# Sixteen rounds of cached value pages in a decoder step: neighbouring rounds, four weight tiles, two row groups

## The chip, the cores and the metric

The kernel runs on one core of a Trainium2 chip. The metric is the time of one launch on the device, in microseconds (us); the time before is the median of three runs. The core has a matrix engine (PE, with its weight loads shown apart as PEld), a vector engine (DVE), an activation engine (ACT), a general engine (POOL) and SyncE (SP), which here only issues transfers. Each engine works through its own queue in order and waits on semaphores.

## The reference

One layer of a decoder step on two groups of tokens at once: a prompt of 256 tokens, and 8 sequences with 4 new tokens each (32 "sample" tokens). 288 tokens in all, 2048 features, float32 throughout.

```
h = h + 1/2 * SwiGLU(RMSNorm(h))                     # FFN 1, hidden 5632
h = h + W_out[ norm(conv group) | norm(attention) ]  # 1024 conv features | 8 heads x 128
h = h + 1/2 * SwiGLU(RMSNorm(h))                     # FFN 2
h = h + sigmoid(W_g RMSNorm(h)) * (W_p p)
y = RMSNorm(h)
```

The attention of the sample tokens runs over a paged past and over the new tokens themselves:

```
k_past = cache_k[page_table]; v_past = cache_v[page_table]     # 8 sequences x 8 pages x 128 rows
s = q k_all^T * SCALE + F_t - F_s                              # forgetting bias, causal
o = softmax(s) @ concat(v_past, v_new)                         # per sequence and head
```

So 64 value pages (128 rows x 8 heads x 128 floats, 512 KB each) have to be gathered and multiplied with the probabilities, and after them the values of the 32 new tokens.

## The kernel before

Activations are kept with features on the 128 partitions and the 288 tokens along the free axis. Each float32 product with a weight is made of three products of a faster type: weight and activation are split into a high and a low part. A weight comes as a block of 512 rows x 256 columns (512 KB, tile `wraw`, tags `raw0` to `raw7`), is split by ACT (`whi`, L271) and DVE (`wlo`, L272) in halves, and one *chunk* of PE work (L304 to L306, 24 matmuls of 288 columns) uses it. `split_upto` keeps five halves ahead of PE.

Weights and value pages are listed in one sequence, `items`. `load_upto` requests them up to a fixed number of items ahead of the point that PE's program has reached (`AHEAD`, 12, in the stage of the pages). Weights are requested on SP's queue (L237), pages as indirect transfers on POOL's queue (L247). A requested tile waits until the former tile of the same tag has been read for the last time. A framework below the kernel places the semaphores, and a planner orders each engine's queue at build time by estimated times: it takes the instruction that is first in the program among those it thinks ready.

*Value pages.* A round `v_round(gi, r)` handles page number `r` (0 to 7) of the four sequences of group `gi` (0 or 1): it has four pages and eight matmuls, two halves `e` of four heads each, by four column tiles of 32 (one a sequence), and adds into two PSUM banks `va`. Rounds are numbered 0 to 15 here, group 0 first, and pages 0 to 63, four a round. There are eight page buffers, taken in turn by `page_tile`: `raw4` to `raw7`, which the weights give up while pages come (`WEIGHTS` is 4), three of their own (`v0` to `v2`) and `wideb`. Page n reuses, in the main, the buffer of page n - 8; at the start the order is shifted, since `wideb` isn't free yet: page 7 takes page 0's buffer, page 11 takes that of page 4 (`v0`).

After round 7 and after round 15 `sample_out` adds the new tokens' part (`vs`, eight matmuls with 32 rows, L750), and DVE picks each head's own rows; `sample_turn` transposes the result (L765). `natural` writes the new tokens' values into `vs` while the value projection runs, and `probs_t` turns the probabilities into `PT`, the weights of the rounds.

*The order.* The chunks of this stage are a list `fill`: 0 to 15 the key projection, 16 to 51 conv, 52 to 67 the value projection, 68 to 79 conv, 80 to 95 the conv half of the output projection. Everything else is hung into it by hand with `at(i, ...)`: it is put before chunk i. Round r stands at `int(51 + 2.7 * r)`: 51, 53, 56, 59, 61, 64, 67, 69, 72, 75, 78, 80, 83, 86, 88, 91. The attention heads of the prompt (`prompt_head`, eight from 69 to 86; their masks on POOL, transposes L814 three chunks later) stand there too. Then the attention half of the output projection follows, and FFN 2.

The weights' tag is chosen as

```
state["wslot"] = (state["wslot"] + 1) % (WEIGHTS if 0 < state["pages"] < 2 * DB * PAGES // 2 else RAW)
```

where `state["pages"]` counts the pages requested so far: from the first page requested to the last one there are four weight tiles, before and after eight.

Of the kernel before, what the change touches and what calls it, by code (L numbers as in the profile page):

```python
# [16 lines left out]
F32 = mybir.dt.float32  # L17
# [79 lines left out]
def build(nc, tc, ctx, A, O):  # L97
# [121 lines left out]

    steps = []  # L220
    items = []
    state = dict(wslot=0, pages=0, ahead=RAW, loaded=0, split=0, used=0, halves_used=0, chunk=0, lead=HALVES)

    def load_upto(n):
        while state["loaded"] < min(n, len(items)):
            it = items[state["loaded"]]
            if it["kind"] == "p" and "vx" not in W:
                return
            if it["kind"] == "w":
                state["wslot"] = (state["wslot"] + 1) % (WEIGHTS if 0 < state["pages"] < 2 * DB * PAGES // 2 else RAW)  # L230
                t = rawp.tile([P, it["nk"], 256], F32, name="wraw", tag=f"raw{state['wslot']}")
                src = it["src"].rearrange("(k p) c -> p k c", p=P)
                if state["loaded"] == 0:
                    tc.keep_in_program_order(sy.dma_start(t[:, :2], src[:, :2]))
                    d = sy.dma_start(t[:, 2:], src[:, 2:])
                else:
                    d = sy.dma_start(t, src)  # L237
                if state["used"] < 24:
                    tc.keep_in_program_order(d)
            elif it["kind"] == "k":  # L240
                t = W["kt"][0].tile([P, 4, NH, P], F32, name="KT", tag="KT", bufs=2)
                for i, r in enumerate(it["rows"]):
                    g.indirect_dma_start(out=t[:, i].rearrange("p h s -> p (h s)"), out_offset=None, in_=it["src"],  # L243
                                         in_offset=bass.IndirectOffsetOnAxis(ap=r, axis=0))
            else:
                t = page_tile()
                g.indirect_dma_start(out=t, out_offset=None, in_=it["src"],  # L247
                                     in_offset=bass.IndirectOffsetOnAxis(ap=it["rows"], axis=0))
            it["tile"] = t
            state["loaded"] += 1  # L250
# [372 lines left out]
    def v_evac(i):  # L623
        def evac(b, o):
            hh = 2 * i + b
            t = W["cv"][0].tile([P, NT], F32, name="tB", tag="tB", bufs=3)
            v.tensor_tensor(t, o, rs, ALU.mult)

            def out():
                c = slice(hh * P, hh * P + P)  # L630
                natural(M["vn"][:, :, c], M["vs"][:, c], t)
            defer(out)
        return evac

# [78 lines left out]
    def probs_t(gi):  # L713
        pt = wide(*(("vv", "c"), ("mix", "a"))[gi], f"PT{gi}")
        x = M["s", gi]
        for j in range(2):
            t = ktbank()
            for i in range(4):
                c = (4 * j + i) * P
                pe.transpose(t[:, i * P:i * P + P], x[:, c:c + P], ident)  # L720
            for b in range(4):
                v.tensor_copy(pt[:, j * 512:j * 512 + 512].rearrange("s (i b c x) -> s b i c x", i=4, b=4, c=4)[:, b],
                              t.rearrange("s (i c b x) -> s b i c x", i=4, c=4, b=4)[:, b])
        t = ktbank()
        pe.transpose(t[:NS, :P], x[:, PAGES * P:], ident)
        for b in range(4):
            v.tensor_copy(pt[:NS, 8 * P + 32 * b:8 * P + 32 * b + 32].rearrange("s (c x) -> s c x", x=8),
                          t[:NS, :P].rearrange("s (c b x) -> s b c x", c=4, b=4)[:, b])
        M["PT", gi] = pt

    def v_round(gi, r):
        its = [page(A["cache_v"], (4 * gi + b) * PAGES + r) for b in range(4)]

        def fn():
            if r == 0:
                M["va", gi] = [bank("va", BANKS["va"]) for _ in range(2)]
                M["pv", gi] = M["PT", gi].rearrange("s (r b x) -> s r b x", b=4, x=32)
            for e in range(2):
                for b in range(4):
                    pe.matmul(M["va", gi][e][32 * b:32 * b + 32, :], M["pv", gi][:, r, b],  # L740
                              its[b]["tile"][:, e * 512:e * 512 + 512], start=r == 0, stop=False, tile_position=(0, 32 * b))
            if r == PAGES - 1:
                sample_out(gi)
        return (its, fn)

    def sample_out(gi):
        mx = W["vv"][0]
        for e in range(2):
            for b in range(4):
                pe.matmul(M["va", gi][e][32 * b:32 * b + 32, :], M["pv", gi][:NS, 8, b],  # L750
                          M["vs"][:, e * 512:e * 512 + 512], start=False, stop=True, tile_position=(0, 32 * b))
        o = mx.tile([P, P], F32, name="so", tag="so", bufs=2)
        for hh in range(NH):
            src = M["va", gi][hh // 4][:, hh % 4 * P:hh % 4 * P + P]
            m = const("headmask")[:, hh:hh + 1]
            if hh == 0:
                v.tensor_scalar(o, src, m, None, ALU.mult)
            else:
                v.scalar_tensor_tensor(o, src, m, o, ALU.mult, ALU.add)
        defer(lambda: sample_turn(gi, o))  # L760

    def sample_turn(gi, o):
        mx = W["vv"][0]
        t = ktbank()
        pe.transpose(t[:, :P], o, ident)  # L765
        for half in range(2):
            v.tensor_copy(M["oS"][:, 4 * half:4 * half + 4, 16 * gi:16 * gi + 16].rearrange("p c (b t) -> p c b t", t=DT),
                          t[:, :P].rearrange("p (b c a t) -> p a c b t", c=4, a=2, t=DT)[:, half])
        if gi == 1:
            s.dma_start(O["v_prompt"].rearrange("(j p) c -> p j c", p=P), M["vn"])  # L770
            s.dma_start(O["v_sample"], M["vs"])
            for hh in range(NH):
                split(za[hh][0][:, SEQ:], za[hh][1][:, SEQ:], M["oS"][:, hh, :], gain("norm_attn_out", hh))
            sq = mx.tile([P, NH, NS], F32, name="sqS")
            s.activation(sq, M["oS"], AF.Square)
            v.tensor_reduce(acc[:, SEQ:], sq.rearrange("p h n -> p n h"), AX.X, ALU.add)
# [130 lines left out]
    def v_start():  # L907
# [5 lines left out]
        state["ahead"] = AHEAD  # L913
        vv = W["vv"][0]
        M["vn"] = vv.tile([P, 2, NH * P], F32, name="vn")
        M["vs"] = vv.tile([NS, NH * P], F32, name="vs")
        M["oS"] = vv.tile([P, NH, NS], F32, name="oS")

    def between(fill, marks):
# [26 lines left out]
    def at(i, *fns):  # L946
        marks.setdefault(i, []).extend(fns)
# [39 lines left out]
    at(50, lambda: probs_t(0))  # L987
    at(52, lambda: probs_t(1))
    for r in range(2 * PAGES):
        at(int(51 + VSTEP * r), v_round(r // PAGES, r % PAGES))  # L990
    for hh in range(NH):
        at(int(69 + 2.5 * hh), lambda hh=hh: prompt_head(hh))
    at(80, lambda: norm_scale(rsc, acc2, CB * P, 2))
# [138 lines left out]
```

## Time and profile before

| what | before |
|---|---|
| median of 3 runs | 2338.74 us (2338.55 to 2339.37) |
| profiled execution | 2338.26 us, its span 2336.5 us |
| granted clock of PE, mean | 0.997 |
| value rounds, L740 | 256 records, first start 1106.9 us, last 1285.5 us |
| new tokens' part, L750 | 32 records, 1184.2 us and 1286.5 us |
| transfers over the span | 443.52 MB, mean 190 GB/s |

A row of the timeline reads: start in us, length in us, engine, line, operation, output<-inputs, shape (rows * columns of weights, then output), count, and in brackets the idle time of the engine before it with what ended it. A row of waits reads: who waited <- for whom: us in total, times, longest. A row of windows reads: stretch, its length, the busy time of each engine with its instructions in brackets, the granted clock, the busy share of the transfer engines and GB/s. A row of a transfer queue reads: packets, MB, share of the 16 engines. A float32 matmul with page data shows as two records, one a pass, so a round of eight matmuls shows as x16.

### The profile page before, as it was taken

Reading aid. Unit: us, or ns where it says so; the run is one execution under the profiler, and the core shown is the slowest. Engines: PE = TensorE matmul, PEld = TensorE weight load, DVE = VectorE, ACT = ScalarE, POOL = GpSimd, SP = SyncE. Lnnn points to the kernel's source line nnn. Section 1 sums busy time; section 2 is a strip of 40 time slices with the busy share of each in tenths; the row PEclk is TensorE's granted clock in tenths of the full one; section 3 lists DMA queues with packets and bytes.
Section 4 is the critical chain, followed back from the end, with each engine's and each line's share of the span. In section 5 each row is a group of like instructions: output and inputs, shape, how many; then the busy total and the mean of one; then the engine's idle time right before and its main releaser. Section 6 shows DMA issues by size and latency. Waiting matters only on the chain.

```text
span 2336.5 us, 44258 instructions
## 1 busy us (share of the span) xinstructions
PE 2319.3 (99%) x17390; PEld 2256.6 (97%) x17390; DVE 1338.8 (57%) x2386; ACT 1054.9 (45%) x1857; POOL 334.0 (14%) x403
## 2 busy tenths in 40 slices
PE   9999999999999999999999999999999999999997
PEld 9999999999999999888888999999999999999997
DVE  6555555555555585455566765555555555555755
ACT  7444444444444553333344554444444444444654
POOL 2020000000000113444445210000000000000111
PEclk9999999999999999999999999999999999999999
DMA  8575555555555557998998455555555555555552
GB/s 273 162 239 164 167 166 163 166 166 165 162 165 167 164 160 230 333 311 260 327 312 284 154 164 156 178 154 174 168 163 163 167 166 164 163 167 166 163 170 86
DMA packets 391089, 443.52 MB, mean 190 GB/s; under 512 B 17104, under 2 KB 371424, under 8 KB 390880
## 3 DMA queue, kind: packets, MB, share of 16 engines
q1 hardware_dynamic: 369456, 366.89, 50.6%
q0 software_dynamic: 20384, 71.38, 8.8%
q8 instruction: 136, 2.23, 0.4%
q10 hardware_dynamic: 1040, 2.42, 0.3%
q14 instruction: 73, 0.60, 0.1%
HBM read 435.56 MB, written 5.07 MB: 189 GB/s over the span
## 4 chain that ended last, share of the span: by engine, by line
PE 99%; DVE 0%; DMA 0%; ACT 0%; DVEq 0%; issue 0%; ACTq 0%
PE mm L304 31%; PE mm L306 31%; PE mm L305 30%; PE va L740 1%; PE va L683 1%; PE va L306 1%; PE va L304 1%; PE va L305 1%; PE kt L180 0%; PE kt L304 0%; PE kt L306 0%; PE kt L305 0%; DVE h L1067 0%; DMA gT<-in_gains_dram 0%; DMA wraw<-in_w_out_dram 0%; PE kt L790 0%
## 5 line engine op out<-in xcount | busy, mean ns | idle before, releaser
L272 DVE TENSOR_TENSOR wlo<-wraw,whi 128x512 fp32r<-128x512 f32 x1384 | 971.5, 706 | 802.4 <-ACT whi L271 749.0
L271 ACT ACTIVATE whi<-wraw 128x512 fp32r<-128x512 f32 x1384 | 865.3, 630 | 948.5 <-PE mm L305 879.3
L304 PE MATMUL mm<-xh,whi 128*128 128x288 f32 x3680 | 1094.8, 297 | 0.0
L305 PE MATMUL mm<-xl,whi 128*128 128x288 f32 x3680 | 1085.6, 295 | 0.0
L306 PE MATMUL mm<-xh,wlo 128*128 128x288 f32 x3680 | 1082.2, 294 | 0.0
L304 PEld LDWEIGHTS mm<-xh,whi 128*128 128x128 f32 x3680 | 689.5, 187 | 23.2 <-issue 20.2
L306 PEld LDWEIGHTS mm<-xh,wlo 128*128 128x128 f32 x3680 | 692.9, 188 | 0.1
L305 PEld LDWEIGHTS mm<-xl,whi 128*128 128x128 f32 x3680 | 690.8, 188 | 0.2
L304 PE MATMUL mm<-hh,whi 128*128 128x288 f32 x1408 | 416.8, 296 | 0.0
L305 PE MATMUL mm<-hl,whi 128*128 128x288 f32 x1408 | 415.4, 295 | 0.0
L306 PE MATMUL mm<-hh,wlo 128*128 128x288 f32 x1408 | 414.0, 294 | 0.0
L370 POOL TENSOR_TENSOR sr<-sg,rs 128x288 f32<-128x288 f32 x88 | 72.4, 823 | 1407.7 <-ACT sg L368 1407.6
L306 PEld LDWEIGHTS mm<-hh,wlo 128*128 128x128 f32 x1408 | 265.2, 188 | 0.0
L305 PEld LDWEIGHTS mm<-hl,whi 128*128 128x128 f32 x1408 | 264.3, 188 | 0.0
L304 PEld LDWEIGHTS mm<-hh,whi 128*128 128x128 f32 x1408 | 263.7, 187 | 0.0
L390 DVE SCALAR_TENSOR_TENSOR h<-mm,h 128x288 f32<-128x288 f32 x192 | 87.2, 455 | 23.3 <-PE mm L306 22.9
L215 POOL TENSOR_TENSOR acc<-acc,sq 128x288 f32<-128x288 f32 x59 | 51.1, 866 | 248.5 <-ACT sq L214 245.6
L243 POOL DMA_INDIRECT KT<-in_cache_k_dram,idx x64 | 66.0, 1032 | 122.7 <-PE va L683 54.2
L368 ACT ACTIVATE sg<-tg 128x288 f32<-128x288 f32 x88 | 39.0, 444 | 97.8 <-DVE tg L366 97.7
L377 ACT ACTIVATE hh<-hd 128x288 fp32r<-128x288 f32 x88 | 39.2, 446 | 92.8 <-DVE hd L375 92.8
L247 POOL DMA_INDIRECT page<-in_cache_v_dram,idx x64 | 64.5, 1008 | 71.3 <-PE va L740 49.4
L378 DVE TENSOR_TENSOR hl<-hd,hh 128x288 fp32r<-128x288 f32 x88 | 40.8, 464 | 22.1 <-ACT hh L377 22.1
(232 smaller groups left out, 1329.9 us busy)
## 6 DMA issues: line engine op xcount, KB each, us to landing
wraw<-in_w_ffn_up_dram SPq DMA_DIRECT2D x176, 512.0 KB
wraw<-in_w_ffn_gate_dram SPq DMA_DIRECT2D x175, 512.0 KB
wraw<-in_w_ffn_down_dram SPq DMA_DIRECT2D x160, 512.0 KB
wraw<-in_w_in_dram SPq DMA_DIRECT2D x96, 512.0 KB
wraw<-in_w_out_dram SPq DMA_DIRECT2D x32, 512.0 KB
wraw<-in_w_ple_gate_dram SPq DMA_DIRECT2D x32, 512.0 KB
wraw<-in_w_ffn_down_dram SPq DMA_DIRECT2D x32, 256.0 KB
wraw<-in_w_ple_proj_dram SPq DMA_DIRECT2D x8, 256.0 KB
```

The costliest lines, as they stand in the source:

```text
L215: (v if k >= KT - last_on_v else g).tensor_tensor(acc, acc, sq, ALU.add)
L243: g.indirect_dma_start(out=t[:, i].rearrange("p h s -> p (h s)"), out_offset=None, in_=it["src"], in_offset=bass.IndirectOffsetOnAxis(ap=r ...
L247: g.indirect_dma_start(out=t, out_offset=None, in_=it["src"], in_offset=bass.IndirectOffsetOnAxis(ap=it["rows"], axis=0))
L271: s.activation(hi, x, AF.Copy)
L272: v.tensor_tensor(lo, x, hi.bitcast(F32), ALU.subtract)
L304: pe.matmul(o, hi[:, j % 2, w], xh, start=f, stop=False)
L305: pe.matmul(o, hi[:, j % 2, w], xl, start=False, stop=False)
L306: pe.matmul(o, lo[:, j % 2, w], xh, start=False, stop=l)
L370: g.tensor_tensor(r, u, rs, ALU.mult)
L377: s.activation(H["hi"][:, k, :], t, AF.Copy)
L378: v.tensor_tensor(H["lo"][:, k, :], t, H["hi"][:, k, :].bitcast(F32), ALU.subtract)
L390: v.scalar_tensor_tensor(h[:, k, :], o, 0.5, h[:, k, :], ALU.mult, ALU.add)
```

## The change

Four edits. Round r of group 0 moves so that rounds 1 and 2, 3 and 4, 5 and 6 stand at one place each, and of group 1 so that 8 and 9, 10 and 11, 12 and 13, 14 and 15 do: 51, 56, 56, 61, 61, 67, 67, 69, then 75, 75, 80, 80, 86, 86, 91, 91. Weights stay on four tiles until the code of the last round has been written (`through`), instead of until the last page has been requested; then they go on with `raw4`. The new tokens' values `vs` are kept with heads 0 to 3 on partitions 0 to 31 and heads 4 to 7 on partitions 32 to 63, the probabilities of the new tokens are copied to both, and the eight matmuls of `sample_out` alternate between the two row groups. The output `v_sample` is therefore written by two transfers. `page_tile`, `AHEAD` and all else are as before.

```diff
--- before.py
+++ after.py
@@ -219,7 +219,7 @@
 
     steps = []
     items = []
-    state = dict(wslot=0, pages=0, ahead=RAW, loaded=0, split=0, used=0, halves_used=0, chunk=0, lead=HALVES)
+    state = dict(wslot=0, pages=0, through=False, ahead=RAW, loaded=0, split=0, used=0, halves_used=0, chunk=0, lead=HALVES)
 
     def load_upto(n):
         while state["loaded"] < min(n, len(items)):
@@ -227,7 +227,7 @@
             if it["kind"] == "p" and "vx" not in W:
                 return
             if it["kind"] == "w":
-                state["wslot"] = (state["wslot"] + 1) % (WEIGHTS if 0 < state["pages"] < 2 * DB * PAGES // 2 else RAW)
+                state["wslot"] = (state["wslot"] + 1) % (WEIGHTS if state["pages"] and not state["through"] else RAW)
                 t = rawp.tile([P, it["nk"], 256], F32, name="wraw", tag=f"raw{state['wslot']}")
                 src = it["src"].rearrange("(k p) c -> p k c", p=P)
                 if state["loaded"] == 0:
@@ -628,7 +628,8 @@
 
             def out():
                 c = slice(hh * P, hh * P + P)
-                natural(M["vn"][:, :, c], M["vs"][:, c], t)
+                r = NS * (hh // 4)
+                natural(M["vn"][:, :, c], M["vs"][r:r + NS, hh % 4 * P:hh % 4 * P + P], t)
             defer(out)
         return evac
 
@@ -723,9 +724,10 @@
                               t.rearrange("s (i c b x) -> s b i c x", i=4, c=4, b=4)[:, b])
         t = ktbank()
         pe.transpose(t[:NS, :P], x[:, PAGES * P:], ident)
-        for b in range(4):
-            v.tensor_copy(pt[:NS, 8 * P + 32 * b:8 * P + 32 * b + 32].rearrange("s (c x) -> s c x", x=8),
-                          t[:NS, :P].rearrange("s (c b x) -> s b c x", c=4, b=4)[:, b])
+        for e in range(2):
+            for b in range(4):
+                v.tensor_copy(pt[NS * e:NS * e + NS, 8 * P + 32 * b:8 * P + 32 * b + 32].rearrange("s (c x) -> s c x", x=8),
+                              t[:NS, :P].rearrange("s (c b x) -> s b c x", c=4, b=4)[:, b])
         M["PT", gi] = pt
 
     def v_round(gi, r):
@@ -740,15 +742,18 @@
                     pe.matmul(M["va", gi][e][32 * b:32 * b + 32, :], M["pv", gi][:, r, b],
                               its[b]["tile"][:, e * 512:e * 512 + 512], start=r == 0, stop=False, tile_position=(0, 32 * b))
             if r == PAGES - 1:
+                if gi == 1:
+                    state.update(through=True, wslot=WEIGHTS - 1)
                 sample_out(gi)
         return (its, fn)
 
     def sample_out(gi):
         mx = W["vv"][0]
-        for e in range(2):
-            for b in range(4):
-                pe.matmul(M["va", gi][e][32 * b:32 * b + 32, :], M["pv", gi][:NS, 8, b],
-                          M["vs"][:, e * 512:e * 512 + 512], start=False, stop=True, tile_position=(0, 32 * b))
+        for b in range(4):
+            for e in range(2):
+                rows = slice(NS * e, NS * e + NS)
+                pe.matmul(M["va", gi][e][32 * b:32 * b + 32, :], M["pv", gi][rows, 8, b], M["vs"][rows], start=False, stop=True,
+                          tile_position=(NS * e, 32 * b))
         o = mx.tile([P, P], F32, name="so", tag="so", bufs=2)
         for hh in range(NH):
             src = M["va", gi][hh // 4][:, hh % 4 * P:hh % 4 * P + P]
@@ -768,7 +773,8 @@
                           t[:, :P].rearrange("p (b c a t) -> p a c b t", c=4, a=2, t=DT)[:, half])
         if gi == 1:
             s.dma_start(O["v_prompt"].rearrange("(j p) c -> p j c", p=P), M["vn"])
-            s.dma_start(O["v_sample"], M["vs"])
+            for e in range(2):
+                s.dma_start(O["v_sample"][:, 512 * e:512 * e + 512], M["vs"][NS * e:NS * e + NS])
             for hh in range(NH):
                 split(za[hh][0][:, SEQ:], za[hh][1][:, SEQ:], M["oS"][:, hh, :], gain("norm_attn_out", hh))
             sq = mx.tile([P, NH, NS], F32, name="sqS")
@@ -913,7 +919,7 @@
         state["ahead"] = AHEAD
         vv = W["vv"][0]
         M["vn"] = vv.tile([P, 2, NH * P], F32, name="vn")
-        M["vs"] = vv.tile([NS, NH * P], F32, name="vs")
+        M["vs"] = vv.tile([2 * NS, NH * P // 2], F32, name="vs")
         M["oS"] = vv.tile([P, NH, NS], F32, name="oS")
 
     def between(fill, marks):
@@ -987,7 +993,7 @@
     at(50, lambda: probs_t(0))
     at(52, lambda: probs_t(1))
     for r in range(2 * PAGES):
-        at(int(51 + VSTEP * r), v_round(r // PAGES, r % PAGES))
+        at(int(51 + VSTEP * (min(PAGES - 1, (r + 1) // 2 * 2) if r < PAGES else r | 1)), v_round(r // PAGES, r % PAGES))
     for hh in range(NH):
         at(int(69 + 2.5 * hh), lambda hh=hh: prompt_head(hh))
     at(80, lambda: norm_scale(rsc, acc2, CB * P, 2))
```

## The prediction

> **What bounds the kernel now.** I read the page first, then the timeline of PE in the stage of the value pages, the waits of the queues there, the DMA counters of short windows and the clock by windows.
>
> ```profile
> PE 2319.3 (99%) x17390; PEld 2256.6 (97%) x17390; DVE 1338.8 (57%) x2386; ACT 1054.9 (45%) x1857; POOL 334.0 (14%) x403
> PE 99%; DVE 0%; DMA 0%; ACT 0%; DVEq 0%; issue 0%; ACTq 0%
> ```
>
> The first line is busy time by engine, the second the chain that ended last. Both are PE for 99%, and after the value pages PE stays the chain: a microsecond won or lost on PE in that stage reaches the end whole. So I look only for what PE spends there.
>
> One isolated round, with the weight loads that show its inner steps:
>
> ```profile
> 1127.62 0.29 PE L305 MATMUL mm<-xl,whi 128*128 128x288 f32 x1
> 1127.76 0.29 PE L306 MATMUL mm<-xh,wlo 128*128 128x288 f32 x1
> 1127.98 1.92 PE L740 MATMUL va<-page,PT 128*32 128x512 f32 x16
> 1129.84 0.40 PE L304 MATMUL mm<-xh,whi 128*128 128x288 f32 x1
> 1130.07 0.29 PE L305 MATMUL mm<-xl,whi 128*128 128x288 f32 x1
> ...
> 1106.92 0.16 PEld L740 LDWEIGHTS va<-page,PT 128*32 128x32 f32 x8 [0.17 <-issue]
> 1107.38 0.13 PEld L740 LDWEIGHTS va<-page,PT 128*32 128x32 f32 x4 [0.30 <-issue]
> 1107.81 0.13 PEld L740 LDWEIGHTS va<-page,PT 128*32 128x32 f32 x4 [0.30 <-issue]
> ```
>
> Starts count here, since ends are modelled. Ordinary matmuls start every 0.133 us (1127.62 to 1127.76), so a chunk of 24 takes 3.2 us. With the round between, L306 to the second matmul after it takes 1130.07 - 1127.76 = 2.31 us where 0.27 would do: an isolated round costs 2.04 us. Inside it the four column tiles of one pass go together, and passes follow at 0.43 us (1107.38 to 1107.81): four passes are 1.72 us, and 0.32 us is the way in and out.
>
> The end of the stage:
>
> ```profile
> 1285.52 1.04 PE L740 MATMUL va<-page,PT 128*32 128x512 f32 x8
> 1286.49 1.92 PE L750 MATMUL va<-vs,PT 32*32 32x512 f32 x16
> 1290.98 0.40 PE L304 MATMUL mm<-zch,whi 128*128 128x288 f32 x1 [2.57 <-ACT whi L271]
> ...
> SPq L237 <- PE va L740: 8.9, 2, 8.0
> ACT whi L271 <- DMA wraw<-in_w_out_dram: 8.9, 1, 8.9
> ...
> 1292.20:1295.60 3.40, 3.40 (x17) 3.40 (x16) 2.49 (x7) 1.59 (x5) 0.80 (x1) 0.50 0.49 166
> 1295.60:1299.00 3.40, 3.40 (x27) 3.40 (x27) 3.31 (x11) 2.90 (x11) 0.81 (x1) 1.00 0.42 142
> ```
>
> PE stands 2.57 us after the last round. It waits for ACT's split of a weight, ACT waits for that weight's DMA, and SP had held its issue 8.0 us until a round freed the tile. The last two lines are windows (the third figure from the end is the granted clock): right behind the stall the clock is 0.50 for 3.4 us.
>
> **The change part by part.**
>
> *Weights on four tiles until the last round.* Today the eight-tile rotation starts when the last page is requested, and weights are then queued on tiles that still hold pages of rounds 14 and 15: this is the 8.0 us wait above. With four tiles they wait only for splits, as everywhere else in the stage, where PE shows no such stall. Gain: 2.57 us, and the half clock: 3.4 us x (1 - 0.133/0.24) = 1.5 us, with 0.24 us the pitch in
>
> ```profile
> 1292.86 0.24 PE mm L305
> 1293.10 0.24 PE mm L306
> ```
>
> from the chain. Together **-4.1 us**. Nothing should follow it: four raw tiles and five split halves hold about six chunks, 19 us, while rounds 14 and 15 with their finish hold PE for 5 us. SP has nothing behind the weights.
>
> *Pairs.* Rounds 1+2, 3+4, 5+6 and 8+9, 10+11, 12+13, 14+15 become neighbours; 0 and 7 stay alone. Each of seven joins saves at most the 0.32 us of one way in and out, and at least 0.18 us, if the passes at a seam keep their first-pass and last-pass gaps (0.46 and 0.53 us for 0.43). A seam of two rounds has one tile shape on both sides, like the seam of the two halves inside a round, so I take the upper: 7 x 0.32 = **-2.2 us** (bounds -1.3 and -2.2).
>
> *New tokens' values on two row groups.*
>
> ```profile
> 1182.37 1.93 PE L740 MATMUL va<-page,PT 128*32 128x512 f32 x16
> 1184.23 1.92 PE L750 MATMUL va<-vs,PT 32*32 32x512 f32 x16
> 1186.08 0.49 PE L789 MATMUL kt<-k,q 128*128 128x128 f32 x2
> ```
>
> The eight matmuls take 1.85 us, four passes of four tiles. If the two row groups go side by side, two passes are left: 2 x 0.43 = 0.86 us less, twice, **-1.7 us**. If they don't, nothing: no row here shows row groups together, so the bounds are 0 and -1.7; I take -1.7, by the four column tiles that do share 0.43 us. [...]
>
> What is added is off PE:
>
> ```profile
> L727 DVE COPY PT<-kt x8: 169/169/169, 1105.0 to 1114.9; 32x32 f32<-32x32 f32 x8
> L771 ACTq DMA_DIRECT2D out_dram<-vs x1: 374/374/374, 1182.8 to 1182.8; - x1
> ```
>
> Eight more of these copies of probabilities on DVE, 4 x 169 ns = 0.7 us a group, behind the copies that the rounds read; and one more output DMA issue of 0.37 us on ACT. DVE is busy 57%, ACT 45%, and five split halves, 8 us of PE's work, cover both. Cost 0.
>
> *What the pairs ask of the pages.* Eight page buffers, and the order in which they are reused is not changed. Page 11 (the fourth of round 2) takes the buffer of page 4 (the first of round 1), tag v0. Today three chunks lie between; now nothing does. How long a page takes:
>
> ```profile
> 1109.11 1.04 POOL L247 DMA_INDIRECT page<-in_cache_v_dram,idx  x1 [7.52 <-PE va L740]
> ...
> q0 software_dynamic: 169, 0.63, 48.0%
> ...
> 1163.16 0.94 POOL L247 DMA_INDIRECT page<-in_cache_v_dram,idx  x1 [6.97 <-PE va L740]
> 1166.89 1.34 POOL L247 DMA_INDIRECT page<-in_cache_v_dram,idx  x1 [0.30 <-issue]
> ...
> q0 software_dynamic: 576, 2.10, 52.7%
> ```
>
> The round that began at 1106.92 released POOL's issue at 1109.11, 2.19 us after its start. The first q0 line is the window 1109.1 to 1113.3: 0.63 MB, so a page (0.52 MB) is in 4.2 us after its issue. The second is 1163.1 to 1174.0: all four pages of a batch (2.10 MB), 10.8 us after the first issue. Hence (10.8 - 4.2) / 3 = 2.2 us for each further page.
>
> Page 11 is then in at 2.19 + 4.2 = 6.4 us after round 1's start; round 2 is due at 1.72. It is 4.7 us late. What PE does meanwhile depends on the planner that orders PE's queue:
>
> ```profile
> 1186.65 0.48 PE L304 MATMUL mm<-xh,whi 128*128 128x288 f32 x1
> ...
> 1190.16 0.29 PE L305 MATMUL mm<-xl,whi 128*128 128x288 f32 x1
> 1190.29 0.27 PE L765 MATMUL kt<-consts,so 128*128 128x128 f32 x1
> 1190.32 0.38 PE L306 MATMUL mm<-xh,wlo 128*128 128x288 f32 x1
> ```
>
> The program puts L765 after 12 matmuls of that chunk; it stands after 26, between two that the program writes as neighbours. So the planner fills a foreseen wait with later matmuls. I expect it to do so in round 2: page 11's two matmuls go into the next chunk, four passes alone, 4 x 0.43 + 0.32 = **+2.0 us** (upper end: PE stands, below).
>
> Round 7 is the other place. Its pages take round 5's buffers; round 5 now runs three steps later, and round 7 is due where it was. Round 6 of today, for the distance to round 7 at 1182.37 above:
>
> ```profile
> 1173.28 1.92 PE L740 MATMUL va<-page,PT 128*32 128x512 f32 x16
> ```
>
> Round 6, two chunks and a head's transposes take 9.1 us, so round 7 is due 1.72 + 9.1 = 10.8 us after round 5 starts. Its pages are in at 2.19 + 10.8 = 13.0. A wait of 2.2 us; I take **+2.2** (bounds: 0, if the pages come at the pace of a less loaded DMA, and 3.7 with the half clock behind it).
>
> The other pairs have five or six chunks. Last of eight pages: 2.2 + 4.2 + 7 x 2.2 = 21.8 us after the pair's first start; due at 2 x 1.72 + 0.3 + 16 + 1.7 = 21.4 before transposes and heads, which add 0.6 us for rounds 3 and 4 and more later. About even, 0 taken. POOL issues eight pages in a row, 10 us at 1.24 us each, with the heads' masks, the adds into h and the squares' sum queued behind; the transposes of a head come three chunks, 9.6 us, after its scores, so the masks come late by about a microsecond at worst and the planner moves the transposes: 0.
>
> Sum: -4.1 - 2.2 - 1.7 + 2.0 + 2.2 = **-3.8 us**. The profiled execution took 2338.26 us (span 2336.5), 0.5 below the median of 2338.74; from the median, **2334.9 us**.
>
> **The rivals.**
>
> *PE stands in order for page 11.* The planner goes by its own times; if it takes the page for ready, the queue keeps program order and PE waits. [...] By rows: 4.7 us of idle instead of 2.0, and since 2.57 us of idle brought the half clock, 1.5 us more: +6.2, sum +0.4, 2339.1 us. The trace agrees where it shows a wait: in the stall at 1288 nothing passed the waiting L304. For the rival: all sixteen rounds of today stand whole (x16) in program order. Against: L765.
>
> *The eight pages of a pair don't come in time (slower).* Place: rounds 4, 11 and 15, five chunks after the pair before. It decides from a page pace of about 2.6 us: then the eighth page is in at 24.6 us, after what heads and transposes add. At 3.0 us a page it is 27.4, some 4 us late, with the half clock 5.5 us, at three places +16: 2351 us; at one place 2340.4. For it: DMA is busy 0.95 to 0.99 there today,
>
> ```profile
> 1120.00:1140.00 20.00, 20.00 (x154) 18.37 (x153) 9.31 (x17) 6.89 (x11) 8.19 (x8) 1.00 0.99 342
> 1140.00:1160.00 20.00, 20.00 (x155) 16.77 (x154) 9.11 (x17) 5.64 (x10) 7.52 (x8) 1.00 0.95 315
> ```
>
> (the last two figures: DMA share, GB/s). Against: the bytes of the stage are unchanged and weights have 19 us of stock to give way.
>
> *The late pages cost nothing.* The planner moves all of round 2's second half behind a chunk and round 7's pages land 2 us earlier. Sum -8.0: 2330.7 us. For it: q0 moves a page in less where weights pause. Against: four passes for one tile alone can't be free.
>
> **How the numbers follow.** A measurement tells 0.2% from no change, 4.7 us: under 2334.1 is faster, over 2343.4 slower. Forecast (planner fills, round 7 waits): 0.50, 2332.5 to 2337; 0.17 of it is under 2334.1. PE stands: 0.20, 2336 to 2342, all same. Pairs starve: 0.15, slower in 0.12. Late pages free: 0.15, faster. Faster 0.32, same 0.56, slower 0.12. Range 2331.0 to 2342.0: below lies half of the free case, above most of the starved one.
>
> **What would show it.** After: no 2.6 us gap behind the last L750 (its line moved), no SP wait of 8 us on L740, clock 1.00 there; L750's successor in two passes, about 1 us; seven L740 groups of x32, or, if the planner fills, six and one of x28 with x4 on its own 2 to 5 us later; a wait of PE for page in round 7. The prediction is wrong if PE waits for page at rounds 4, 11 or 15, or if the row groups don't overlap.

## The result, and the profile after

The changed kernel took 2348.64 us (median of six, 2345.27 to 2351.89), the kernel before 2339.30 in the same comparison (2338.55 to 2339.97): a ratio of 1.0042, 95% interval 1.0032 to 1.0052. The forecast was 2334.9 with a range to 2342.0. So it is slower by 9.3 us, and 13.7 above the forecast. The runs of the changed kernel also lie 6.6 us apart, those of before 1.4. The profiled execution took 2351.89 us (span 2350.1).

The page, busy time and chain:

```profile
PE 2323.0 (99%) x17390; PEld 2260.1 (96%) x17390; DVE 1337.9 (57%) x2394; ACT 1054.7 (45%) x1857; POOL 331.6 (14%) x403
PE 98%; DVE 0%; issue 0%; DMA 0%; ACT 0%; another core or an unknown queue 0%; DVEq 0%; SPq 0%
```

PE still carries the chain and its count of instructions is unchanged; but a point of its share is gone, and busy ends are modelled, so the loss has to be looked for in starts. First the places that the prediction named, in PE's timeline:

```profile
1126.20 3.63 PE L742 MATMUL va<-page,PT 128*32 128x512 f32 x28
...
1132.50 1.90 PE L742 MATMUL va<-page,PT 128*32 128x512 f32 x4 [0.75 <-DMA page<-in_cache_v_dram,idx]
...
1149.82 0.29 PE L306 MATMUL mm<-xh,wlo 128*128 128x288 f32 x1
1150.04 3.64 PE L742 MATMUL va<-page,PT 128*32 128x512 f32 x32
1153.61 0.40 PE L304 MATMUL mm<-xh,whi 128*128 128x288 f32 x1
1153.85 0.29 PE L305 MATMUL mm<-xl,whi 128*128 128x288 f32 x1
...
1305.24 1.09 PE L755 MATMUL va<-vs,PT 32*32 32x512 f32 x16
1306.26 0.40 PE L304 MATMUL mm<-zch,whi 128*128 128x288 f32 x1
```

All edits did on PE what their steps said: a pair is one group of x32; rounds 1 and 2 are x28 with page 11's x4 later; the new tokens' values take 1.02 us (1305.24 to 1306.26) for 1.85; and behind the last round there is no gap. SP's wait for tiles that pages held is 1.5 us for 8.9:

```profile
SPq L237 <- PE va L742: 1.5, 2, 0.8
```

Then windows, first the three stretches of half clock, then the whole stage (the third figure from the end is the granted clock):

```profile
1187.60:1191.00 3.40, 3.40 (x19) 2.47 (x22) 1.53 (x5) 0.63 (x1) 0.00 (x0) 0.50 1.03 406
1262.70:1266.10 3.40, 3.40 (x16) 3.22 (x15) 2.50 (x8) 1.04 (x3) 2.30 (x4) 0.50 0.49 154
1290.00:1293.40 3.40, 3.40 (x17) 3.38 (x16) 3.24 (x6) 2.34 (x6) 1.23 (x2) 0.50 1.02 388
1100.00:1330.00 230.00, 217.80 (x1606) 187.19 (x1605) 130.76 (x310) 87.74 (x182) 94.69 (x115) 0.98 0.79 264
```

The one half-clock stretch of before, behind the last round, has become three at other places. PE's own waits in the stage (line, releaser, us in total, times, longest):

```profile
PE mm L304 <- issue: 2.5, 3, 1.1
PE kt L617 <- issue: 2.3, 1, 2.3
...
PE va L742 <- DMA page<-in_cache_v_dram,idx: 0.8, 1, 0.8
```

PE waits 0.8 us for pages in all. The larger waits are under "issue": nothing that the profile shows. One such place, behind the pair of rounds 3 and 4, on PE, ACT, DVE and POOL:

```profile
1148.89 0.29 PE L305 MATMUL mm<-xl,whi 128*128 128x288 f32 x1
...
1155.84 0.29 PE L305 MATMUL mm<-xl,whi 128*128 128x288 f32 x1
...
1159.04 0.29 PE L305 MATMUL mm<-xl,whi 128*128 128x288 f32 x1
...
1161.04 0.29 PE L305 MATMUL mm<-xl,whi 128*128 128x288 f32 x1
1161.47 0.29 PE L306 MATMUL mm<-xh,wlo 128*128 128x288 f32 x1
1162.91 0.39 PE L304 MATMUL mm<-xh,whi 128*128 128x288 f32 x1 [1.15 <-issue]
```

```profile
1149.22 0.63 ACT L271 ACTIVATE whi<-wraw 128x512 fp32r<-128x512 f32 x1 [2.40 <-PE mm L305]
1150.07 0.63 ACT L271 ACTIVATE whi<-wraw 128x512 fp32r<-128x512 f32 x1 [0.21 <-PE mm L305]
1158.24 0.63 ACT L271 ACTIVATE whi<-wraw 128x512 fp32r<-128x512 f32 x1 [7.54 <-PE mm L306]
1160.10 0.63 ACT L271 ACTIVATE whi<-wraw 128x512 fp32r<-128x512 f32 x1 [1.23 <-PE mm L306]
1163.81 2.20 ACT L271 ACTIVATE whi<-wraw 128x512 fp32r<-128x512 f32 x4 [3.07 <-PE mm L306]
```

```profile
1158.90 0.69 DVE L272 TENSOR_TENSOR wlo<-wraw,whi 128x512 fp32r<-128x512 f32 x1 [7.48 <-PE mm L306]
```

```profile
1152.22 0.94 POOL L247 DMA_INDIRECT page<-in_cache_v_dram,idx  x1 [14.18 <-PE va L742]
1153.46 0.94 POOL L247 DMA_INDIRECT page<-in_cache_v_dram,idx  x1 [0.30 <-issue]
...
1160.93 1.41 POOL L247 DMA_INDIRECT page<-in_cache_v_dram,idx  x1 [0.30 <-PE mm L306]
```

How to read them. Five split halves (whi and wlo) go round; ACT may write a whi once PE has read the one five before for the last time, which is an L305, the 17th or 23rd matmul of an undivided chunk. Undisturbed, ACT starts 0.33 us after that matmul starts: 1148.89, 1149.22. Behind the pair the matmul is at 1155.84 and ACT starts at 1158.24: 2.40 us. Weights were not short: the one split at 1160.10 had landed by 1148.2. Two splits later the delay is 4.77 us (the L305 at 1159.04, whi at 1163.81). The row says the same by the name it gives: the releaser should be L305, and where it is L306, PE had gone on to later matmuls before ACT was let go. The trace's record of PE's semaphore says it too: an undisturbed release is on record 0.31 us after the start of its matmul; here four fall due between 1156.1 and 1157.1, and none is on record before 1157.88. POOL's run of eight requests lasts from 1152.22 to 1162.34, just over this time. PE itself makes no progress from 1161.04 to 1162.91 but for one matmul, and not for want of halves: the two of its chunk were split by 1159.59 (ACT at 1150.07 and 1158.24, DVE's wlo at 1158.90), and the row names no one. The totals of that wait for the stage, before and after:

```profile
ACT whi L271 <- PE mm L306: 6.4, 5, 2.2
```

```profile
ACT whi L271 <- PE mm L306: 31.6, 10, 7.5
```

### The profile page after: what moved, and what is told of

Same layout as the page of the kernel before. It is cut to its first block, busy times and chain, and to the rows that moved or that the text cites. A ratio compares the mean times of both kernels' runs of the same rounds, so it can differ in the third digit from the quotient of the medians.

```text
span 2350.1 us, 44277 instructions
## 1 busy us (share of the span) xinstructions
PE 2323.0 (99%) x17390; PEld 2260.1 (96%) x17390; DVE 1337.9 (57%) x2394; ACT 1054.7 (45%) x1857; POOL 331.6 (14%) x403
## 4 chain that ended last, share of the span: by engine, by line
PE 98%; DVE 0%; issue 0%; DMA 0%; ACT 0%; another core or an unknown queue 0%; DVEq 0%; SPq 0%
PE mm L304 31%; PE mm L306 30%; PE mm L305 30%; PE va L684 1%; PE va L742 1%; PE va L304 1%; PE va L306 1%; PE va L305 1%; DMA h<-in_x_dram 0%; PE kt L796 0%; PE kt L304 0%; PE kt L306 0%; PE kt L305 0%; DVE h L1073 0%; PE kt L180 0%
## 5 line engine op out<-in xcount | busy, mean ns | idle before, releaser
L305 PE MATMUL mm<-xl,whi 128*128 128x288 f32 x3680 | 1086.1, 295 | 0.5 <-issue 0.5
L306 PE MATMUL mm<-xh,wlo 128*128 128x288 f32 x3680 | 1082.6, 294 | 0.1
L306 PEld LDWEIGHTS mm<-xh,wlo 128*128 128x128 f32 x3680 | 693.3, 188 | 0.7 <-issue 0.7
L305 PEld LDWEIGHTS mm<-xl,whi 128*128 128x128 f32 x3680 | 691.1, 188 | 0.9 <-issue 0.7
L305 PE MATMUL mm<-hl,whi 128*128 128x288 f32 x1408 | 415.4, 295 | 0.0
L306 PE MATMUL mm<-hh,wlo 128*128 128x288 f32 x1408 | 414.0, 294 | 0.0
L306 PEld LDWEIGHTS mm<-hh,wlo 128*128 128x128 f32 x1408 | 265.1, 188 | 0.0
L305 PEld LDWEIGHTS mm<-hl,whi 128*128 128x128 f32 x1408 | 264.2, 188 | 0.0
```

Source lines behind the costliest of these rows:

```text
L305: pe.matmul(o, hi[:, j % 2, w], xl, start=False, stop=False)
L306: pe.matmul(o, lo[:, j % 2, w], xh, start=False, stop=l)
```

## The experiments

Theory: the run of eight page requests that a pair sets free on POOL delays PE's releases of split halves. Rivals: the long round starves the splits by itself; masks and head steps stand behind the pages on POOL; the four-tile rotation starves them. Each run was timed beside the kernel before, which stood at 2338.3 to 2338.8 us.

One thing that is no edit sorts these runs. In the key stage (900 to 1100 us) POOL asks for key pages by a list, four in a row, and no edit touches it. Yet ACT's waits for PE differ there, here in the changed kernel and in the run with the later transposition:

```profile
ACT whi L271 <- PE mm L305: 84.5, 69, 3.8
ACT whi L271 <- PE mm L306: 13.3, 7, 2.3
```

```profile
ACT whi L271 <- PE mm L305: 109.4, 89, 3.8
```

Counted in the traces, nine kernels have 35 to 44 of 219 releases by ordinary matmuls in this stage late or missing on record (none within 0.45 us of the matmul's start). They are the kernel before, the changed kernel, and the runs marked *late* below. In the eleven runs marked *prompt* it is none of 218 to 222. Runs made at one time are alike, so this came with the occasion and not with the kernel. What it is, no run shows, and the changed kernel itself has no run with prompt releases. A difference between a *late* and a *prompt* run can therefore not be put down to the edit.

**The two small edits without pairs** (changed kernel, places of before).

```diff
-    at(int(51 + VSTEP * (min(PAGES - 1, (r + 1) // 2 * 2) if r < PAGES else r | 1)), v_round(...))
+    at(int(51 + VSTEP * r), v_round(r // PAGES, r % PAGES))
```

> The changed kernel with its rounds back at the old sixteen places (no pairs): weights on four tiles until the last round, and new tokens' values on two row groups, remain. All theories: the two terms stand by themselves, -4.1 and -1.7 us, so 2339.3 - 5.8 = 2333.5 us, and the stretches in which PE's releases reach ACT late (2 to 5 us for 0.33) are gone. If the four-tile rotation itself starves the splits, it is 2339 or more.

Measured (*late*): 2334.20 us, ratio 0.9979 (0.9970 to 0.9988). The stalls are gone, so the pairs carry the loss and the rotation doesn't. Of the 5.8 us, 4.6 arrived. A wait behind round 7 is about as large as the rest, in PE's, DVE's and ACT's timelines of this run:

```profile
1188.50 0.29 PE L305 MATMUL mm<-xl,whi 128*128 128x288 f32 x1
...
1192.56 0.30 PE L770 MATMUL kt<-consts,so 128*128 128x128 f32 x1 [1.36 <-DVE pst L812]
```

```profile
1191.46 0.69 DVE L272 TENSOR_TENSOR wlo<-wraw,whi 128x512 fp32r<-128x512 f32 x1 [1.38 <-ACT whi L271]
1192.07 0.34 DVE L764 SCALAR_TENSOR_TENSOR so<-va,consts,so 128x128 f32<-128x128 f32 x1
```

```profile
1190.80 0.63 ACT L271 ACTIVATE whi<-wraw 128x512 fp32r<-128x512 f32 x1 [1.41 <-PE mm L306]
```

The transposition of the sample outputs (L770) waits for DVE's last add into so, queued behind a split that itself waited for ACT. And ACT waited for a late release: the L305 it needed started at 1188.50, 2.30 us before whi.

**Pairs alone** (kernel before with the new places).

> The kernel before with the rounds in pairs and nothing else. If the pairs alone carry the loss: 2348.6 + 5.8 = 2354.4 us. If the loss needs the four-tile rotation beside the pairs (rival): 2335 to 2340.

Measured (*late*): 2355.97, ratio 1.0070 (1.0054 to 1.0085). The pairs cost 17 us by themselves.

**Seven pages.**

```diff
+            elif state["pages"] >= 7:
+                t = kept[state["pages"] % 7]
+                state["pages"] += 1
```

> The changed kernel, but only the first seven value pages are loaded and every later round multiplies one of these seven tiles: 57 page transfers and their issues on POOL are left out, PE's work and the pairs stay. Theory (the eight pages asked for in one run behind a pair hold up the releases of the split buffers): the stalls go, 2348.6 - 12 to 16 = 2333 to 2336 us or a little less, and the delay from the needed matmul to the next split is 0.33 us everywhere. Rival 1 (3.4 us of page matmuls in one piece starve or misorder the splits by themselves): 2346 to 2349. Rival 2 (masks and head steps queue behind the pages on POOL): the stalls of group 1 go, those of group 0 at 1161 and 1184 stay, about 2341.

Measured (*late*, and yet no release of the value stage is late): 2330.27, ratio 0.9961 (0.9946 to 0.9976). PE's work in pairs is the same, so the long round alone is not the cause. The stalls of both groups go. Masks would be free of pages here too, but at the place shown above POOL holds the eight requests and nothing else, so they are not the cause there.

**Four and four.**

```diff
+                if state["pages"] in (16, 24, 32, 44, 52, 60):
+                    if state["chunk"] < state["hold"]:
+                        return
+                    d, j = halves[state["split"] - 1]
+                    g.tensor_copy(held, d["parts"][j][1][0:1, 0, 0:1].bitcast(F32))
```

(hold is set two chunks ahead by each second round of a pair.)

> The changed kernel, with the second four of the eight pages behind each pair held on POOL until a weight's second split two chunks later is made (a copy of one element that waits for it). Bytes, pairs and PE's work are unchanged; eight requests in a row become four and four. Theory (the run of eight): half or more of the 13 us of stalls go, 2338 to 2343 us. Rival 1 (the long round itself): 2347 to 2350. Rival 2 (masks behind pages): no better than 2347, since the masks now wait longer.

Measured (*late*): 2342.91, ratio 1.0016 (1.0007 to 1.0025): not quite half of the stalls went; those about round 7 remain.

**Requests without bytes, half the bytes, bytes without POOL, requests without a list.** Four runs that change one thing of the request each:

```diff
-                g.indirect_dma_start(out=t, out_offset=None, in_=it["src"], ...)
+                g.indirect_dma_start(out=t[:, :8], ..., in_=it["src"].rearrange("r (c e) -> (r c) e", e=8), ...)   # 32 bytes a row; 512 for half
+                sy.dma_start(t, it["src"][j * P:j * P + P])    # SP
+                g.dma_start(t, it["src"][j * P:j * P + P])     # POOL, plain
```

> The changed kernel with all 64 requests of value pages on POOL at their places, but from the eighth on each brings 128 rows of 32 bytes instead of 4096, into the first columns of one of seven loaded tiles: the values of these pages are left out. Issues and descriptors stay, the bytes go. If POOL's run of eight issues by itself delays PE's releases: 2344 to 2349 us, and delays of 2 to 5 us behind the pairs remain. If the eight transfers' bytes do: about as with seven pages, 2330 to 2333 us, and delays of 0.33.

> As the run with 32 bytes a row, with 2048 bytes a row instead of 4096: POOL's issues and descriptors as in the changed kernel, half the bytes (the values of pages from the eighth on are left out). If the stalls come once transfers last longer than POOL takes to ask for the next (1.24 us an issue; a whole page takes about 2 us of the queue, half a page about 1), so that requests pile up: no stalls, 2331 to 2334 us. If any sizeable bytes behind POOL's requests do it: in between, 2337 to 2345.

> The changed kernel with its value pages loaded by SP's queue as plain transfers of the same size, in the order of the pool and not by the page table (the lookup is left out). The bytes and the times at which buffers come free stay, POOL issues nothing. If the bytes of eight pages in a run delay PE's releases: 2344 to 2349 us. If POOL's issuing does: 2330 to 2336 us. A queue of weights behind pages on SP would show as waits for wraw's DMA, and would add to either.

> The changed kernel with its value pages still requested by POOL, eight in a row behind a pair, but as plain transfers of 128 rows in the order of the pool, without a list of rows (the lookup by the page table is left out). So far POOL's requests without bytes (2332.0) and the bytes without POOL's requests (2333.9) both lose the stalls. If what delays PE's releases is a run of transfers whose descriptors POOL writes, lookup or not: 2344 to 2349 us. If it is the lookup of the rows in particular: 2331 to 2336.

Measured (all four *prompt*): 2332.01 without bytes (0.9971, 0.9960 to 0.9982), 2331.86 with half (0.9971, 0.9960 to 0.9982), 2333.87 from SP (0.9980, 0.9971 to 0.9990), 2333.64 plain from POOL (0.9978, 0.9968 to 0.9987). None has the stalls. But none has a late release anywhere, so they don't tell whether issues, bytes or the list carry the loss. Besides, the pages of the first two go round seven tiles and not eight, which also changes what some requests wait for; and a run of plain requests is much shorter on POOL (eight in one row):

```profile
1152.64 4.18 POOL L248 DMA_DIRECT2D page<-in_cache_v_dram  x8 [17.03 <-PE va L742]
```

**With a list, in the pool's order**, since the plain runs read other places in memory too.

```diff
+                                     in_offset=bass.IndirectOffsetOnAxis(ap=seq[:, j:j + 1], axis=0))
```

> The changed kernel, its pages requested with a list of rows as there, but the list counts the rows of the pool in order, as the plain transfers read them (2333.6 us), instead of the page table's. If the list (POOL works 0.94 us on such a request, 0.53 on a plain one) makes the difference: 2345 to 2350 us. If the places in memory do: 2332 to 2336.

Measured (*late*): 2348.69, ratio 1.0043 (1.0026 to 1.0060). Beside the 2348.64 with the page table's list, the places in memory make no difference here.

**Plain requests stretched.**

```diff
+                    g.tensor_copy(held, C[:, 0:FILL])
```

> The run with plain requests (no list of rows, pool order, 2333.6 us) with a copy of 192 columns on POOL ahead of each from the ninth on, so that eight requests last about 9 to 10 us instead of 4. If the length of POOL's run beside the transfers delays PE's releases, list or not: 2344 to 2350 us. If it is the list: 2333 to 2336.

Measured (*prompt*): 2345.76, ratio 1.0031 (1.0021 to 1.0042). It answers nothing. The copies ran at the kernel's start (27.0 to 57.9 us), the requests kept their pace (POOL's timeline; 2.65 us for five), and the time went at the start too (PE's timeline), far from the pages:

```profile
1141.00 2.65 POOL L252 DMA_DIRECT2D page<-in_cache_v_dram  x5 [8.76 <-PE va L746]
```

```profile
60.04 0.61 PE L308 MATMUL mm<-xh,whi 128*128 128x288 f32 x1 [7.11 <-ACT whi L275]
```

**Copies that wait for nothing**, written ahead of each request of the changed kernel.

```diff
+                if state["pages"] >= 8:
+                    g.tensor_copy(held, C[0:1, 0:1])
```

> The changed kernel with a copy of one element on POOL ahead of each page request from the ninth on; nothing waits for the copies and they wait for nothing. If requests standing back to back on POOL delay PE's releases: 2332 to 2340 us. If it is the number of requests within ten microseconds, with their bytes: 2345 to 2350.

Measured (*late*): 2349.15, ratio 1.0048 (1.0031 to 1.0064). It answers nothing either: all 56 copies ran at the kernel's start (27.4 to 49.5 us), so behind rounds 3 and 4 the eight requests stand in a row as before, 1.25 to 1.36 us apart. It is the changed kernel once more, and took the same.

**Two requests a chunk** in the changed kernel; then the same holding with **pairs at other places** (0 and 1 alone, 2+3 to 14+15, group 0's transposition one chunk later), then that **without the holding**, then **with waits but no holding**.

```diff
+                if m >= 12 and m % 2 == 0 and m != 28:
+                    if state["chunk"] < state["hold"] and state["loaded"] - state["used"] > 4:
+                        return
+                    state["hold"] = state["chunk"] + 1
+                    d, j = halves[state["split"] - 1]
+                    g.tensor_copy(held, d["parts"][j][1][0:1, 0, 0:1].bitcast(F32))
...
+        at(int(51 + VSTEP * (r if r < 2 else r | 1)), v_round(r // PAGES, r % PAGES))
+        defer(lambda: sample_turn(gi, o), 2 - gi)
```

> The changed kernel with the pages asked for two at a time, one pair of requests for each chunk (held on POOL by a copy of one element that waits for a split), instead of eight in a row. By the theory that the run of eight carries the loss, by its bytes or by its issues: 2332 to 2337 us, below the 2342.9 of four and four. If a pair's long stretch on PE is what matters beside any transfer: no better than four and four, 2341 to 2345. If the last two pages come too late for their pair, waits of PE for page appear and it is over 2340.

> A version for use: the two small edits, group 0's transposition one chunk later, rounds 2+3, 4+5, ... 14+15 in pairs (0 and 1 alone, so that no page's buffer is wanted by the round next to it), and pages from round 4 on asked for two at a time, one pair of requests a chunk. Theory: seven joins at 0.32 us on top of the 2332.35 us of the same without pairs, 2330.1 us, and delays of 0.33. If holding the requests makes the last pages late, PE waits for page: 2332 to 2336. If long rounds cost by themselves: above 2333.

> The version of 2330.6 us (pairs 2+3 to 14+15) without the holding of requests: eight in a row again. If the run of eight carries the loss wherever the pairs stand: 2340 to 2348 us. If the places of the pairs (page 11's buffer, round 7 alone) carry it: 2330 to 2333.

> The version with pairs 2+3 to 14+15 and eight requests in a row (2350.5 us), with a copy of one element ahead of each request from round 4 on that waits for the latest split then written in the program; no request is kept for a later chunk, and most of these waits are over when POOL comes to them. If what counts is that requests come at least a split apart, as in the held version: 2340 to 2350. If the mere wait ahead of a request does it (POOL's sequencer can't run ahead): 2330 to 2334.

Measured: 2335.55 (*prompt*; 0.9986, 0.9977 to 0.9996); 2330.64 (*prompt*; 0.9967, 0.9955 to 0.9979); 2350.49 (*late*; 1.0050, 1.0033 to 1.0067); 2330.77 (*prompt*; 0.9965, 0.9953 to 0.9978). The third is 20 us above the second, but one is *late* and the other *prompt*, so this is not the price of the copies and their waits. Its stall has the form of the one above (ACT; the matmul it needed started at 1148.25), so the loss doesn't hang on where the pairs stand:

```profile
1152.66 0.63 ACT L272 ACTIVATE whi<-wraw 128x512 fp32r<-128x512 f32 x1 [6.49 <-PE mm L307]
```

The fourth has only the copies of the last experiment below, from page 16 on, and no hold. The planner put them ahead of each run: behind rounds 4 and 5 eight list requests follow each other at 1.24 to 1.32 us with no copy between (1163.56 to 1172.38), and no release is late. So such a run does not delay releases in every case.

**Later transposition** (two small edits, L770 one chunk later) and **four tiles alone** (kernel before and the rotation edit).

```diff
-        defer(lambda: sample_turn(gi, o))
+        defer(lambda: sample_turn(gi, o), 2 - gi)
```

> The kernel with the two small edits alone (2334.2 us), and group 0's transposition of the sample outputs put one chunk later: there PE stood 1.66 us for DVE, whose last add into so was queued behind a split. If this wait is what the shorter finish lost: 2334.2 - 1.4 = 2332.8 us. If the wait only moves to the next work that needs DVE: 2334.

> The kernel before with the weights on four tiles until the last round and nothing else. By the prediction's term: 2338.7 - 4.1 = 2334.6 us. The two small edits together came to 2334.2, so if this is 2334.6 the row groups gave 0.4 of their 1.7 net, the rest being the wait for so; if it is 2336 the four tiles are worth less than their term.

Measured (both *prompt*): 2332.35 (0.9974, 0.9964 to 0.9983) and 2334.46 (0.9982, 0.9973 to 0.9991). The first can't be held against the 2334.20 of the same kernel without the shift, which is *late*.

**The changed kernel with waits ahead of its requests**, nothing moved.

```diff
+                if state["pages"] >= 12:
+                    d, j = halves[state["split"] - 1]
+                    g.tensor_copy(held, d["parts"][j][1][0:1, 0, 0:1].bitcast(F32))
```

> The changed kernel, nothing moved, with a copy of one element on POOL ahead of each page request from round 3 on that waits for the latest weight split then written in the program. If the way in which POOL's requests follow a pair carries the whole loss: 2348.6 - 13 = 2333 to 2337 us, and no delays of 2 to 5 us behind the pairs. If the places of the pairs (page 11's buffer, round 7 alone) carry part of it: 2338 to 2345. If waits ahead of the requests help only at the other places: 2346 or more.

Measured (*prompt*): 2335.07, ratio 0.9984 (0.9975 to 0.9993). The place shown above, in this run's PE, POOL and ACT:

```profile
1150.66 3.64 PE L746 MATMUL va<-page,PT 128*32 128x512 f32 x32
...
1156.46 0.29 PE L309 MATMUL mm<-xl,whi 128*128 128x288 f32 x1
```

```profile
1148.46 1.35 POOL L249 COPY held<-wlo 1x1 f32<-1x1 f32 x6 [9.89 <-DVE wlo L276]
...
1152.92 0.96 POOL L251 DMA_INDIRECT page<-in_cache_v_dram,idx  x1 [0.57 <-PE va L746]
1154.19 0.94 POOL L251 DMA_INDIRECT page<-in_cache_v_dram,idx  x1 [0.30 <-issue]
...
1162.28 0.18 POOL L249 COPY held<-wlo 1x1 f32<-1x1 f32 x1
1162.62 0.96 POOL L251 DMA_INDIRECT page<-in_cache_v_dram,idx  x1 [0.16 <-PE mm L310]
```

```profile
1157.13 1.15 ACT L275 ACTIVATE whi<-wraw 128x512 fp32r<-128x512 f32 x2 [5.81 <-PE mm L310]
1160.05 1.37 ACT L275 ACTIVATE whi<-wraw 128x512 fp32r<-128x512 f32 x2 [1.77 <-PE mm L309]
```

Six of the copies are taken before the run. It starts 2.26 us after the pair, against 2.18, goes at nearly the same pace, and its last request starts 1 us later; yet ACT comes 0.67 us after its matmul and not 2.40. The window of the whole stage:

```profile
1100.00:1330.00 230.00, 227.95 (x1726) 199.06 (x1725) 146.39 (x334) 97.85 (x201) 110.91 (x171) 1.00 0.82 275
```

PE begins 120 matmul records more in the same 230 us (1726 for 1606) and the clock stays whole (1.00 for 0.98). At 0.133 us each that is 16 us; the two profiled spans differ by 15.8 (2350.1 and 2334.3). Whether the copies did this or the occasion is not shown: this run has prompt releases in the key stage too, and in four and four, where such copies stood ahead of six requests, the releases stayed late.

## Why the prediction was wrong

The step that failed is the last one of "What the pairs ask of the pages": "POOL issues eight pages in a row, 10 us at 1.24 us each", taken at 0. It asked what stands behind the pages on POOL (masks, adds into h) and found those covered. What was delayed beside the run is on other engines: PE's releases, which reached ACT 2.4 to 4.8 us after the matmul instead of 0.33, and PE itself, which stood. Among the *late* runs the kernel took 2348.64 us with the pairs and 2334.20 without, so the pairs cost 14.4 us where the sum had 2.0 (-2.2 + 2.0 + 2.2). With the 1.2 us by which the two small edits fell short there (4.6 for 5.8), this is the whole miss.

The other steps:

- *Four tiles, -4.1.* Right: alone 2338.78 to 2334.46, -4.3.
- *Row groups, -1.7.* Right on PE: 1.02 us for 1.85 at each finish. In the run without pairs, group 0's gain went into the wait for so, behind a late release. With prompt releases, and L770 a chunk later, the two edits are worth 6.3 us (2338.61 to 2332.35) for 5.8; how much of the rest is L770's was not parted.
- *Pairs, -2.2.* The size of a join was right: from L306 at 1149.82 to the second matmul after the pair (1153.85) are 4.03 us where 0.27 would do, 3.76 for two rounds, and 2 x 2.04 - 3.76 = 0.32. In time, among *prompt* runs, seven joins (at the other places) brought 2332.35 to 2330.64, 1.7 us.
- *Page 11, +2.0.* The planner filled as forecast (x28, a half chunk, x4); its guess of the landing was still early, so 0.75 us of wait came on top, 1.16 in the last run.
- *Round 7, +2.2.* Too dear. In the changed kernel PE was itself late there. Where it was not, in the last run, the wait was half a microsecond:

```profile
1185.08 1.06 PE L746 MATMUL va<-page,PT 128*32 128x512 f32 x6
1186.64 1.90 PE L746 MATMUL va<-page,PT 128*32 128x512 f32 x10 [0.50 <-DMA page<-in_cache_v_dram,idx]
```

- *Pages in time.* Right: PE doesn't wait for page at rounds 4, 11 or 15. So the rival that ended slower named the right burst, eight pages at once, and the wrong path: it looked for a late page, and what came late was a release. Its price at three places, +16 us, is near the measured one by chance.
- *PE stands in order for page 11* did not happen: the order that the planner had written was another. In the trace nothing passed page 11's x4 while it waited 0.75 us.

The last run comes out as the sum did, 2335.07 for 2334.9, and partly by luck: page 11 cost 1.2 us more than forecast, round 7 1.7 less.

Shown, then, among the *late* runs: the loss needs the pairs and the requests for their pages, and it is smaller when a run is cut in two; neither the places in memory nor those of the pairs make it. The share of late or missing releases in the value stage (1100 to 1330 us) goes with the run: 41 to 47 of 197 to 221 where eight requests stand in a row, 24 to 27 of 220 to 238 where four do, none of 244 with seven pages. Not shown is why list requests go with late releases in some runs and with prompt ones in others, and what in the chip holds the release. Nor is it shown what takes the loss away: the waits on POOL through the whole stage, fewer bytes, SP as the issuer and plain requests were all run with prompt releases alone. Running the changed kernel again together with these would tell. The copies besides change two things at once: POOL waits for DVE ahead of requests, and later splits wait for POOL's copy of the half they overwrite.

The best version is the one with pairs 2+3 to 14+15 and held requests, 2330.64 us: 8.1 us below before, with the same without holding (2330.77) level with it. Both times are with prompt releases; the same pairs with late ones, and without the copies, took 2350.49. The stage of the best version:

```profile
1100.00:1330.00 230.00, 229.73 (x1761) 203.53 (x1760) 148.88 (x342) 100.70 (x206) 108.86 (x145) 1.00 0.82 278
```

## What to carry to other kernels

When an edit lets more buffers come free at once, ask what the burst of requests does while it lasts, to every engine that hands buffers round, and not only what stands behind it on its queue. A release is a step with a duration: take the normal time from a needed instruction to its follower (0.33 us here) and look for places where it grows; a releaser named one instruction too late in the waits is a hint of it. Take that time also in a stretch that no edit touches: where it differs there between two runs (13.3 us put down to L306 against none in the key stage), the runs differ in more than the edit. And when an engine finishes a step sooner, see who is next in its chain: 0.83 us saved on PE met an add on DVE that was queued behind a split.

## What was not expected of the hardware

- In the changed kernel's runs of eight list requests, releases from PE to ACT came 2.4 to 4.8 us after the matmul instead of 0.33, while the matmuls themselves went on at 0.133 us; in the end PE stopped too, 1.44 us (1161.47 to 1162.91) without a wait that the profile shows.
- Beside list requests whose code is the same, 35 to 44 of 219 releases were late or missing on record in nine kernels and none in eleven others.
- POOL asks for a page by a list every 1.24 us and for a plain one of the same size every 0.52 (4.18 us for eight).
- Row groups and column tiles do go side by side: eight matmuls of 32 rows in 1.02 us for 1.85.
- The granted clock went to 0.50 for 3.4 us soon after some gaps of PE: in the changed kernel the gap of 2.6 us at 1184.30 was followed by it at 1187.6; in the run without pairs the one of 1.7 us at 1190.90 by none (mean granted clock of that run 0.998; of before, with its one such stretch, 0.997).
